# Reading a product's bank before, instead of after, the side work of its period

## Chip, cores and metric

The kernel runs on one core of a Trainium2 chip. The metric is the device time of one launch in microseconds (us). Three runs of the kernel before took 2329.98, 2333.09 and 2333.73 us, median 2333.09.

## What is computed

One layer of a hybrid decoder trunk on a sequence of 2048 tokens of width 1024, all in float32:

```
h = rms_norm(x, pre_norm_w)
p = h @ w_in                       # 1024 x 8320: rwkv, conv, pool, gate columns
y_a = rwkv7_branch(token_shift(p_rwkv, mu_shift), ...)
y_b = b * conv3(c * u) * silu(z)             # p_conv -> b, c, u, z
y_c = mix(window means of u, widths 2..16) * pool_scale * silu(z)
proj = einsum('nbsc,ncd->nbsd', [y_a, y_b, y_c], w_branch)   # 3 x (512 -> 1024)
merged = sum_n sigmoid(p_gate)_n * proj_n
out = x + rms_norm(merged @ w_out, post_norm_w)
```

The rwkv branch is a recurrence over tokens. The kernel solves it in 16 groups of 128 tokens, each with a small triangular inverse.

## The kernel before, in words

The wide matrix products are cut into *products*: one PSUM bank of 128 x 512, twelve TensorE matmuls (four slices of the inner dimension, each as high x high, high x low, low x high halves of a split float32; lines 182 to 184). There are 608 products. Most belong to a `Pair` (lines 189 to 263): two 128-column blocks times two 512-token blocks with seven products instead of eight, called here B11, T1, T2, B21, B22, T3, T4. T4 is postponed and runs inside the next pair, after its T1. There are two `ch` banks and two `mm` banks. B11 is copied out of `ch` by ScalarE (L233), T1 out of `mm` (L238), T2 out of `ch` (L243); B21, B22 and T3 are added by VectorE to these copies (L247, L251, L255). A product may start only when the bank that it writes has been read: T4 needs L255 of T3, two products earlier; T1 of the next pair takes the bank that L247 read.

The weights of a product are split into a high half (ScalarE, `wh`, L141) and a low half (GpSimd, `wl`, L143) a few products ahead, by `supply`; GpSimd also adds weight blocks (L212).

The program runs in *periods*, one to a product: `execute` (lines 1280 to 1299) iterates the job, and at each `yield` behind a product it calls `supply`, issues postponed stores, does one postponed piece of row work (`puts`), and advances the side streams, one step each. Side streams are the rwkv groups, the staging of the second half's operands, the pooled mix, and the splitting of stored activations (`fill`, lines 354 to 358). Only then is the bank read. Each engine works its queue in the order of issue, so the order in which Python issues instructions is the order of each engine's queue.

Names that the prediction needs:
- An rwkv group step by step: G and BK tables; then the *table chain* (L752 to L757), fifteen pairs of small VectorE operations (L754, L755) in four *chunks* over four periods; its result goes to memory and back (L763, L766), is transposed (L771, Td), and TensorE needs Td one period later (L779). VectorE's L794 feeds TensorE's L805 in the same way. L626 belongs to a group's head.
- The merge stage: each product's bank is read by L1015; beside it `fill` (L357 ScalarE, L358 VectorE) prepares later operands.
- The final stage: eight `out_pair`s (lines 1036 to 1073). A row tile needs both its halves: ScalarE squares them (L1049), GpSimd makes the norm (`rstd`, L490 to L492), VectorE scales (L1059) and adds x (L1060). This scaling is postponed through `puts`, except for the T4 half, which is done at once.

Of the kernel before, what the change touches and what calls it, by code (L numbers as in the profile page):

```python
# [53 lines left out]
def trunk_kernel(ctx, tc, x, pre_norm_w, post_norm_w, w_in, mu_shift, rwkv_w0, rwkv_w_up,  # L54
# [39 lines left out]
    def mm_bank():  # L94
        return ps.tile([P, BLK], F32, tag="mm", name="mm", bufs=2)
# [88 lines left out]
            pe.matmul(bank, lo[:, k, :], th[k], start=False, stop=stop and k == HK - 1, skip_group_check=True)  # L184

    sums = [pool]
    tail = [None]

    class Pair:
# [37 lines left out]
        def run(self):  # L227
            ops, sink = self.ops(), self.sink
            ch = chain_bank()
            product(ch, take(), ops["B11"], True)  # L230
            yield
            p1 = work("p1")
            act.copy(p1[:, 16:], ch)  # L233
            bb = mm_bank()
            product(bb, take(), ops["T1"], True)
            yield
            p5 = work("p5")
            act.copy(p5[:, 16:], bb)  # L238
            yield from flush()
            product(ch, take(), ops["T2"], False)  # L240
            yield
            u2 = work("u2")
            act.copy(u2[:, 16:], ch)  # L243
            b2 = mm_bank()
            product(b2, take(), ops["B21"], True)
            yield
            dve.tensor_tensor(p1[:, 16:], p1[:, 16:], b2, ALU.add)  # L247
            sink(0, 0, p1[:, 16:], p1)
            product(bb, take(), ops["B22"], False)
            yield  # L250
            dve.tensor_tensor(u2[:, 16:], u2[:, 16:], bb, ALU.add)  # L251
            sink(0, 1, u2[:, 16:], u2)
            product(ch, take(), ops["T3"], False)
            yield
            dve.tensor_tensor(p5[:, 16:], p5[:, 16:], ch, ALU.add)  # L255
            sink(1, 1, p5[:, 16:], p5)

            def last():
                product(ch, take(), ops["T4"], False)
                yield  # L260
                sink(1, 0, ch, None)

            tail[0] = last
# [25 lines left out]
    def single(ops, c, sink):  # L289

        def body():
            h = ops()
            a1, a2 = take(), take()
            ba, bb = mm_bank(), mm_bank()
            product(ba, a1, h["B11"], True)
            yield
            p1 = work("p1")
            act.copy(p1[:, 16:], ba)  # L298
            product(bb, a1, h["T1"], True, False)
            yield  # L300
            product(ba, a2, h["B21"], False)
            yield
            first = sink(0, ba)
            product(bb, a2, h["B22"], False)
            yield
            dve.tensor_tensor(p1[:, 16:], p1[:, 16:], bb, ALU.add)
            second = sink(1, p1[:, 16:])
            up = take()
            yield from first(up)
            yield from second(up)  # L310

        return Other([w_block(w_in, q, c) for q in range(2)], body)
# [4 lines left out]
    stores, puts = [[], []], []  # L317
# [9 lines left out]
    def after_product():  # L327
        for dst, src in stores.pop(0):
            sp.dma_start(dst, src)
        stores.append([])  # L330
        if puts:
            puts.pop(0)()


    def new_op(o):
# [189 lines left out]
    def rwkv_single(half, h, c):  # L525

        up = []

        def load_up():
            up.append(wp.tile([P, HK, P], F32, tag="ws", name="up", bufs=6))  # L530
            for n, w in enumerate((rwkv_w_up, rwkv_a_up)):
                sp.dma_start(up[0][half_of(n)], w[0].rearrange("k (i n) -> k i n", i=NCT))

        def sink(b, val):
            t0 = half * TH + b * BLK
            sh = rwkv_cols(half, c, b, val)
            th, tl = [wk.tile([P, BLK + 16], F32R, tag="wk", name=t)[:, :BLK] for t in ("th", "tl")]
            act.copy(th, sh)
            dve.tensor_tensor(tl, sh, th.bitcast(F32), ALU.subtract)

            def products(upw):
                (uh, ul) = upw
                for n, bias in enumerate((hw0, ha0)):
                    ns = half_of(n)
                    for i in range(NCT):
                        bank = chain_bank() if i % 2 else mm_bank()
                        pe.matmul(bank, uh[ns, i, :], th[ns], start=True, stop=False)
                        pe.matmul(bank, uh[ns, i, :], tl[ns], start=False, stop=False)
                        pe.matmul(bank, ul[ns, i, :], th[ns], start=False, stop=True)
                        o = work("lo")[:, :BLK]  # L550
                        act.activation(o, bank, AF.Tanh, bias=bias[:, i:i + 1], scale=0.5)
                        store(loraD[n][:, i, t0:t0 + BLK], o)
                        if i == 1:
                            yield
                    yield
            return products

        job = single(h, c * P, sink)
        job.feed.append((load_up, None, lambda: wsplit(up[0])))
        return job  # L560
# [442 lines left out]
    def merge_tile(half, ys, d):  # L1003

        def body():
            acc = [None] * NB
            for n in (1, 2, 0):
                gs = gates()
                w = take()
                turn[0] = not turn[0]  # L1010
                for b in range(NB):
                    bank = mm_bank() if turn[0] else chain_bank()
                    product(bank, w, ys[n, b], True)
                    yield
                    dve.scalar_tensor_tensor(gs[b], gs[b], 1.0, bank, ALU.add, ALU.mult)  # L1015
                    if acc[b] is None:
                        acc[b] = gs[b]
                    else:
                        pool.tensor_tensor(acc[b], acc[b], gs[b], ALU.add)  # L1019
            for b in range(NB):  # L1020
                t0 = half * TH + b * BLK
                store(mD[:, d, t0:t0 + BLK], acc[b])

        return Other([w_block(w_branch[n], 0, d * P) for n in (1, 2, 0)], body)
# [207 lines left out]
    for half in range(2):  # L1232
        side = groups[half]
# [36 lines left out]
    for entry in program:  # L1270
        if isinstance(entry, tuple):
            j = entry[0]
# [7 lines left out]
    def execute(first):  # L1280
        for n, entry in enumerate(program):
            if (n == 0) != first:
                continue
            if not isinstance(entry, tuple):
                entry()
                continue
            j, sides = entry
            if hasattr(j, "begin"):
                j.begin()
            for _ in j.run():  # L1290
                supply(1)
                after_product()
                for side in sides:
                    side.advance()
        if not first:
            for _ in flush():
                after_product()
            while puts or stores[0] or stores[1]:
                after_product()

    with tc.manual_schedule(engines={mybir.EngineType.PE, mybir.EngineType.DVE, mybir.EngineType.Activation,
# [27 lines left out]
```

## Time and profile before

| | |
|---|---|
| median of 3 runs | 2333.09 us |
| profiled run, its own time | 2330.51 us |
| its span | 2328.8 us |
| TensorE busy, share | 2185.9 us, 94% |
| VectorE busy | 1374.5 us, 59% |
| GpSimd busy | 1365.0 us, 59% |
| ScalarE busy | 895.0 us, 38% |
| mean granted TensorE clock | 0.96 |
| share of TensorE in the chain that ended last | 63%, VectorE 14% |

The stages follow each other: preparation up to about 60 us, the first half's products with rwkv groups 0 to 7 up to about 1060 us, the second half's with groups 8 to 15 up to about 1930 us (the merges begin inside it, at about 1838 us), the second half's merges up to 2133 us, the final stage up to the end. The time that counts is TensorE's idle time and the stretches in which its clock is granted at half; the busy shares of the other engines are means over stages.

### The profile page before, as it was taken

The numbers are of one execution on the slowest core, as the hardware profiler recorded it, in microseconds if no ns is written. First come the engines' busy times: TensorE is split into PE (matmuls) and PEld (weight loads), VectorE is DVE, ScalarE is ACT, GpSimd is POOL, SyncE is SP. The second block draws the span as 40 slices with busy tenths as digits, with TensorE's granted clock in tenths as the row PEclk, the third lists the DMA queues.
The fourth block names the chain that finished last, engine by engine and source line by source line (L and its number), as shares of the span: only waits on it lengthen the run. The fifth ranks groups of instructions, "written<-read, shape, count | busy, mean of one in ns | idle before, by whom it ended". The sixth has DMA issues, their size and how long they took to land.

```text
span 2328.8 us, 46956 instructions
## 1 busy us (share of the span) xinstructions
PE 2185.9 (94%) x18514; PEld 1759.5 (76%) x18514; DVE 1374.5 (59%) x2150; ACT 895.0 (38%) x1777; POOL 1365.0 (59%) x1137
## 2 busy tenths in 40 slices
PE   4999999989999999899989999999999999999897
PEld 4788777777787887768877787777877788787775
DVE  7413767676847637534576767846465653526554
ACT  5444433443434436344534433244343511314332
POOL 7657565665656555427656655446565355556775
PEclk7989999999999999979999999999999999999998
DMA  3244313253547427344432323346454765768443
GB/s 103 90 136 129 98 54 95 61 144 107 152 140 209 129 80 236 92 146 138 136 80 62 91 53 113 108 138 186 131 166 118 231 174 170 258 182 275 126 136 104
DMA packets 441207, 313.11 MB, mean 134 GB/s; under 512 B 105557, under 2 KB 362778, under 8 KB 440986
## 3 DMA queue, kind: packets, MB, share of 16 engines
q1 hardware_dynamic: 440986, 310.12, 44.5%
q8 instruction: 145, 2.38, 0.4%
q14 instruction: 76, 0.62, 0.1%
HBM read 206.08 MB, written 103.94 MB: 133 GB/s over the span
## 4 chain that ended last, share of the span: by engine, by line
PE 63%; DVE 14%; issue 5%; POOL 4%; DMA 4%; ACT 3%; SPq 1%; DVEq 0%; POOLq 0%; ACTq 0%
PE ch L182 10%; PE ch L183 9%; PE ch L184 9%; PE mm L182 8%; PE mm L183 7%; PE mm L184 7%; DVE Tt L755 3%; DVE Ttmp L754 3%; PE rk L593 2%; PE rk L711 2%; POOL wl L143 2%; POOL ws L212 1%; PE rk L835 1%; PE rk L827 1%; PE rk L843 1%
## 5 line engine op out<-in xcount | busy, mean ns | idle before, releaser
L143 POOL TENSOR_TENSOR wl<-ws,wh 128x512 fp32r<-128x512 f32 x484 | 674.0, 1395 | 548.1 <-ACT wh L141 514.0
L141 ACT CAST wh<-ws 128x512 fp32r<-128x512 f32 x484 | 298.7, 618 | 253.8 <-PE mm L183 91.3
L182 PE MATMUL ch<-hT,wh 128*128 128x512 f32 x864 | 358.0, 414 | 38.1 <-DVE p L255 30.9
L184 PE MATMUL ch<-hT,wl 128*128 128x512 f32 x864 | 344.8, 399 | 0.3 <-POOL wl L143 0.2
L183 PE MATMUL ch<-lT,wh 128*128 128x512 f32 x864 | 344.9, 399 | 0.1
L182 PE MATMUL mm<-hB,wh 128*128 128x512 f32 x600 | 241.6, 403 | 2.8 <-ACT p L298 2.8
L184 PE MATMUL mm<-hB,wl 128*128 128x512 f32 x600 | 234.3, 390 | 0.7 <-POOL wl L143 0.7
L183 PE MATMUL mm<-lB,wh 128*128 128x512 f32 x600 | 234.3, 391 | 0.0
L182 PEld LDWEIGHTS ch<-hT,wh 128*128 128x128 f32 x864 | 167.5, 194 | 83.3 <-issue 32.6
L143 POOL TENSOR_TENSOR wl<-s,wh 128x512 fp32r<-128x512 f32 x72 | 97.5, 1354 | 217.7 <-ACT wh L141 214.0
L212 POOL TENSOR_TENSOR ws<-ws,s 128x512 f32<-128x512 f32 x144 | 201.7, 1401 | 2.6 <-DMA ws<-in_w_in 2.6
L184 PEld LDWEIGHTS ch<-hT,wl 128*128 128x128 f32 x864 | 166.6, 193 | 38.1 <-POOL wl L143 1.3
L183 PEld LDWEIGHTS ch<-lT,wh 128*128 128x128 f32 x864 | 167.6, 194 | 32.5 <-issue 0.4
L1019 POOL TENSOR_TENSOR g<-g 128x512 f32<-128x512 f32 x64 | 86.4, 1353 | 108.0 <-DVE g L1015 95.9
L182 PEld LDWEIGHTS mm<-hB,wh 128*128 128x128 f32 x600 | 112.6, 188 | 29.7 <-ACT p L298 3.6
L182 PE MATMUL mm<-hT,wh 128*128 128x512 f32 x296 | 124.5, 421 | 10.6 <-DVE p L247 7.0
L184 PEld LDWEIGHTS mm<-hB,wl 128*128 128x128 f32 x600 | 112.7, 188 | 25.8 <-POOL wl L143 1.5
L183 PEld LDWEIGHTS mm<-lB,wh 128*128 128x128 f32 x600 | 112.7, 188 | 21.5
L184 PE MATMUL ch<-hB,wl 128*128 128x512 f32 x288 | 117.7, 409 | 10.5 <-POOL wl L143 10.5
L182 PE MATMUL ch<-hB,wh 128*128 128x512 f32 x288 | 120.8, 419 | 6.8 <-DVE g L1015 4.0
L755 DVE TENSOR_TENSOR Tt<-Tt,Ttmp 128x120 f32<-128x120 f32 (+14 forms) x240 | 117.4, 489 | 8.3
L184 PE MATMUL mm<-hT,wl 128*128 128x512 f32 x296 | 119.9, 405 | 1.0 <-POOL wl L143 0.8
(269 smaller groups left out, 4638.7 us busy)
## 6 DMA issues: line engine op xcount, KB each, us to landing
ws<-in_w_in SPq DMA_DIRECT2D x260, 256.0 KB
g<-gD SPq DMA_DIRECT2D x96, 256.0 KB
gD<-p SPq DMA_DIRECT2D x48, 256.0 KB
ly<-yD SPq DMA_DIRECT2D x48, 256.0 KB
ws<-in_w_branch SPq DMA_DIRECT2D x48, 256.0 KB
mD<-g SPq DMA_DIRECT2D x32, 256.0 KB
ws<-mD SPq DMA_DIRECT2D x32, 256.0 KB
xr<-in_x SPq DMA_DIRECT2D x32, 256.0 KB
```

The source lines that it names most:

```text
L141: act.copy(hi, src)
L143: pool.tensor_tensor(lo, src, hi.bitcast(F32), ALU.subtract)
L182: pe.matmul(bank, hi[:, k, :], th[k], start=start and k == 0, stop=False, skip_group_check=True)
L183: pe.matmul(bank, hi[:, k, :], tl[k], start=False, stop=False, skip_group_check=True)
L184: pe.matmul(bank, lo[:, k, :], th[k], start=False, stop=stop and k == HK - 1, skip_group_check=True)
L212: sums[0].tensor_tensor(w[o], w[a], w[b], op)
L593: both(lambda h, hs: pe.matmul(bank[hs, a * 64:a * 64 + 64], src[hs, a], ident[hs, hs], start=True, stop=True))
L711: both(lambda h, hs: pe.matmul(bgs[n][hs, i * P:(i + 1) * P], BK[hs, n, 2 * i + c], XA[hs, 2 * i + c].rearrange("p x t -> p (x t)"), start ...
L754: dve.tensor_tensor(tmp[:, :, :n], bc(NBt[:, j, j + 1:], 1, 8), bc(Tt[:, :, j], 2, n), ALU.mult)
L755: dve.tensor_tensor(Tt[:, :, j + 1:], Tt[:, :, j + 1:], tmp[:, :, :n], ALU.add)
L827: both(lambda h, hs: pe.matmul(r3[hs, i], G[hs, 1, 0, a], vt[hs, a], start=True, stop=False, skip_group_check=True))
L1019: pool.tensor_tensor(acc[b], acc[b], gs[b], ALU.add)
```

## The change

`yield READ` is put behind each reading of a bank. `execute` now takes two kinds of yields: behind a product it calls `supply` and issues postponed stores, as before; behind the reading it advances the side streams and does one postponed piece of row work. At the end, the loop that empties `puts` does so outside `after_product`, and the two yields of the last T4 do nothing.

```diff
+    READ = True
...
             p1 = work("p1")
             act.copy(p1[:, 16:], ch)
+            yield READ
             bb = mm_bank()
             product(bb, take(), ops["T1"], True)
             yield
...
             yield
             dve.tensor_tensor(p5[:, 16:], p5[:, 16:], ch, ALU.add)
+            yield READ
             sink(1, 1, p5[:, 16:], p5)
 
             def last():
                 product(ch, take(), ops["T4"], False)
                 yield
+                yield READ
                 sink(1, 0, ch, None)
...
         stores.append([])
-        if puts:
-            puts.pop(0)()
...
-                    else:
+                    yield READ
+                    if acc[b] is not gs[b]:
                         pool.tensor_tensor(acc[b], acc[b], gs[b], ALU.add)
...
-            for _ in j.run():
-                supply(1)
-                after_product()
-                for side in sides:
-                    side.advance()
+            for read in j.run():
+                if read:
+                    for side in sides:
+                        side.advance()
+                    if puts:
+                        puts.pop(0)()
+                else:
+                    supply(1)
+                    after_product()
         if not first:
             for _ in flush():
-                after_product()
+                pass
             while puts or stores[0] or stores[1]:
+                if puts:
+                    puts.pop(0)()
                 after_product()
```

The order of instructions on TensorE, GpSimd and the DMA queue is the same as before; only VectorE's and ScalarE's queues change. In the changed kernel the lines are shifted: L247, L251, L255 are L252, L257, L262; L754 and L755 are L767 and L768; L771 is L784; L1059 and L1060 are L1073 and L1074.

VectorE in the final stage, from one pair's B21 (first row) to the next T4's half (last two rows), before:

```order
L247 TENSOR_TENSOR p_22748<-p_22748,mm 128x512
L251 TENSOR_TENSOR u_22820<-u_22820,mm 128x512
L1059 SCALAR_TENSOR_TENSOR p_22748<-p_22748,so,post 128x512
L1060 TENSOR_TENSOR xr<-xr,p_22748 128x512
L255 TENSOR_TENSOR p_22771<-p_22771,ch 128x512
L1059 SCALAR_TENSOR_TENSOR u_22820<-u_22820,so,post 128x512
L1060 TENSOR_TENSOR xr<-xr,u_22820 128x512
L1059 SCALAR_TENSOR_TENSOR o<-ch,so,post 128x512
L1060 TENSOR_TENSOR xr<-xr,o 128x512
```

The same pair with the change:

```order
L252 TENSOR_TENSOR p_22746<-p_22746,mm 128x512
L257 TENSOR_TENSOR u_22818<-u_22818,mm 128x512
L262 TENSOR_TENSOR p_22771<-p_22771,ch 128x512
L1073 SCALAR_TENSOR_TENSOR p_22746<-p_22746,so,post 128x512
L1074 TENSOR_TENSOR xr<-xr,p_22746 128x512
L1073 SCALAR_TENSOR_TENSOR u_22818<-u_22818,so,post 128x512
L1074 TENSOR_TENSOR xr<-xr,u_22818 128x512
L1073 SCALAR_TENSOR_TENSOR o<-ch,so,post 128x512
L1074 TENSOR_TENSOR xr<-xr,o 128x512
```

The reading of T3's bank (L255, now L262) has moved in front of the first postponed scaling.

VectorE at the end of the program, the last pair from T3 on, before:

```order
L255 TENSOR_TENSOR p_23109<-p_23109,ch 128x512
L1059 SCALAR_TENSOR_TENSOR u_23154<-u_23154,so,post 128x512
L1060 TENSOR_TENSOR xr<-xr,u_23154 128x512
L1059 SCALAR_TENSOR_TENSOR o<-ch,so,post 128x512
L1060 TENSOR_TENSOR xr<-xr,o 128x512
L1059 SCALAR_TENSOR_TENSOR p_23109<-p_23109,so,post 128x512
L1060 TENSOR_TENSOR xr<-xr,p_23109 128x512
```

And with the change:

```order
L262 TENSOR_TENSOR p_23109<-p_23109,ch 128x512
L1073 SCALAR_TENSOR_TENSOR p_23086<-p_23086,so,post 128x512
L1074 TENSOR_TENSOR xr<-xr,p_23086 128x512
L1073 SCALAR_TENSOR_TENSOR o<-ch,so,post 128x512
L1074 TENSOR_TENSOR xr<-xr,o 128x512
L1073 SCALAR_TENSOR_TENSOR u_23152<-u_23152,so,post 128x512
L1074 TENSOR_TENSOR xr<-xr,u_23152 128x512
L1073 SCALAR_TENSOR_TENSOR p_23109<-p_23109,so,post 128x512
L1074 TENSOR_TENSOR xr<-xr,p_23109 128x512
```

The scaling of the second half row (`u`) has moved behind the one that waits for T4 (`o`).

VectorE at the start of group 14's table chain, in the pair with T3's reading L255, before:

```order
L251 TENSOR_TENSOR u_18428<-u_18428,mm 128x512
L754 TENSOR_TENSOR Ttmp<-NB,Tt 128x8x15
L755 TENSOR_TENSOR Tt<-Tt,Ttmp 128x8x15
L754 TENSOR_TENSOR Ttmp<-NB,Tt 128x8x14
L755 TENSOR_TENSOR Tt<-Tt,Ttmp 128x8x14
L754 TENSOR_TENSOR Ttmp<-NB,Tt 128x8x13
L755 TENSOR_TENSOR Tt<-Tt,Ttmp 128x8x13
L754 TENSOR_TENSOR Ttmp<-NB,Tt 128x8x12
L755 TENSOR_TENSOR Tt<-Tt,Ttmp 128x8x12
L255 TENSOR_TENSOR p_18334<-p_18334,ch 128x512
```

And with the change:

```order
L257 TENSOR_TENSOR u_18395<-u_18395,mm 128x512
L672 TENSOR_TENSOR d<-d,gst 128x512
L262 TENSOR_TENSOR p_18310<-p_18310,ch 128x512
L767 TENSOR_TENSOR Ttmp<-NB,Tt 128x8x15
L768 TENSOR_TENSOR Tt<-Tt,Ttmp 128x8x15
L767 TENSOR_TENSOR Ttmp<-NB,Tt 128x8x14
```

The reading of T3's bank now stands in front of the chain's first chunk.

## Rows read from the trace of the kernel before

**Rows 1.** Waits of TensorE: in total us, times, longest us

```profile
PE ch L182 <- DVE p L255: 30.9, 13, 5.4
PE rk L779 <- DVE Td L771: 10.8, 5, 3.8
PE rk L805 <- DVE T L794: 9.5, 5, 5.8
PE mm L182 <- DVE p L247: 7.0, 2, 3.5
```

**Rows 2.** Timeline, VectorE, final stage: start, us, operation, [idle before <-releaser]

```profile
2177.89 0.67 DVE L251 TENSOR_TENSOR u<-u,mm 128x512 f32<-128x512 f32 x1
2181.78 1.77 DVE L1059 SCALAR_TENSOR_TENSOR p<-p,so,post 128x512 f32<-128x512 f32 x1 [3.21 <-POOL so L492]
...
2185.14 0.67 DVE L255 TENSOR_TENSOR p<-p,ch 128x512 f32<-128x512 f32 x1
```

**Rows 3.** Timeline, TensorE, T4 of the second out pair

```profile
2185.96 0.52 PE L182 MATMUL ch<-hT,wh 128*128 128x512 f32 x1 [2.62 <-DVE p L255]
```

**Rows 4.** Timeline, GpSimd, the two idle times of the following cycle

```profile
2187.23 1.28 POOL L143 TENSOR_TENSOR wl<-s,wh 128x512 fp32r<-128x512 f32 x1 [2.56 <-ACT wh L141]
...
2201.77 1.30 POOL L143 TENSOR_TENSOR wl<-ws,wh 128x512 fp32r<-128x512 f32 x1 [2.55 <-ACT wh L141]
```

**Rows 5.** Windows: length, busy us (count) PE, PEld, DVE, ACT, POOL; clock; DMA

```profile
2208.39:2230.78 22.39, 19.64 (x84) 15.61 (x85) 11.63 (x12) 7.92 (x19) 16.96 (x17) 1.00 0.49 141
2311.89:2328.80 16.91, 4.36 (x13) 3.19 (x12) 6.36 (x10) 2.52 (x8) 1.87 (x6) 0.72 0.20 75
```

**Rows 6.** Timeline, VectorE, the end

```profile
2311.38 0.68 DVE L251 TENSOR_TENSOR u<-u,mm 128x512 f32<-128x512 f32 x1
...
2315.64 0.68 DVE L255 TENSOR_TENSOR p<-p,ch 128x512 f32<-128x512 f32 x1
...
2325.00 0.69 DVE L1060 TENSOR_TENSOR xr<-xr,p 128x512 f32<-128x512 f32 x1
```

**Rows 7.** Timeline, TensorE, the last T4

```profile
2316.47 0.77 PE L182 MATMUL ch<-hT,wh 128*128 128x512 f32 x1 [4.58 <-DVE p L255]
```

**Rows 8.** Timeline, VectorE, around L626 in a group's head

```profile
247.91 1.76 DVE L626 TENSOR_TENSOR f<-f,k 128x512 f32<-128x512 f32 x1
```

**Rows 9.** Timeline, TensorE, the T4 behind it

```profile
250.42 0.47 PE L182 MATMUL ch<-hT,wh 128*128 128x512 f32 x1 [3.37 <-DVE p L255]
```

**Rows 10.** Timeline, VectorE, group 0's chain in the convolution's pairs

```profile
299.12 0.68 DVE L247 TENSOR_TENSOR p<-p,mm 128x512 f32<-128x512 f32 x1
...
302.91 0.68 DVE L255 TENSOR_TENSOR p<-p,ch 128x512 f32<-128x512 f32 x1
```

**Rows 11.** Timeline, TensorE, T1 and then T4 behind them

```profile
299.94 0.77 PE L182 MATMUL mm<-hT,wh 128*128 128x512 f32 x1 [3.52 <-DVE p L247]
...
305.20 0.54 PE L182 MATMUL ch<-hT,wh 128*128 128x512 f32 x1
```

**Rows 12.** Timeline, VectorE, group 14's chain: first operation, last operation, Td

```profile
1777.65 0.58 DVE L754 TENSOR_TENSOR Ttmp<-NB,Tt 128x120 f32<-128x120 f32 x1
...
1797.73 0.17 DVE L755 TENSOR_TENSOR Tt<-Tt,Ttmp 128x8 f32<-128x8 f32 x1
...
1805.00 0.71 DVE L771 STREAM_TRANSPOSE Td<-TT 128x512 f32<-128x512 f32 x1 [4.70 <-DMA TT<-td]
```

**Rows 13.** Timeline, TensorE: T3's last matmul there, and the matmuls on Td

```profile
1779.29 0.39 PE L184 MATMUL ch<-hT,wl 128*128 128x512 f32 x1
...
1805.77 0.75 PE L779 MATMUL rk<-Td,G 16*32 16x32 f32 x64 [2.27 <-DVE Td L771]
```

**Rows 14.** Timeline, VectorE, splitting activations during the merges

```profile
2005.10 5.78 DVE L358 TENSOR_TENSOR ly<-ly,hy 128x512 fp32r<-128x512 f32 x4
```

**Rows 15.** Timeline, TensorE, the merge product behind it

```profile
2011.61 0.47 PE L182 MATMUL mm<-hy,wh 128*128 128x512 f32 x1 [3.29 <-DVE g L1015]
```

**Rows 16.** Line L754: operation, xcount, duration ns min/median/max, first and last start

```profile
L754 DVE TENSOR_TENSOR Ttmp<-NB,Tt x240: 172/243/1381, 278.0 to 1888.2; 128x120 f32<-128x120 f32 x8, 128x104 f32<-128x104 f32 x8, 128x88 f32<-128x88 f32 x8, 128x72 f32<-128x72 f32 x8
```

More of the change, by code (lines that the diff above doesn't have):

```diff
@@ L251, in run @@
             dve.tensor_tensor(u2[:, 16:], u2[:, 16:], bb, ALU.add)
+            yield READ
             sink(0, 1, u2[:, 16:], u2)
@@ L255, in run @@
             dve.tensor_tensor(p5[:, 16:], p5[:, 16:], ch, ALU.add)
+            yield READ
             sink(1, 1, p5[:, 16:], p5)
@@ L260, in last @@
                 yield
+                yield READ
                 sink(1, 0, ch, None)
@@ L298, in body @@
             act.copy(p1[:, 16:], ba)
+            yield READ
             product(bb, a1, h["T1"], True, False)
             yield
+            yield READ
             product(ba, a2, h["B21"], False)
             yield
+            yield READ
             first = sink(0, ba)
@@ L306, in body @@
             dve.tensor_tensor(p1[:, 16:], p1[:, 16:], bb, ALU.add)
+            yield READ
             second = sink(1, p1[:, 16:])
@@ L554, in products @@
                             yield
+                            yield READ
                     yield
+                    yield READ
             return products
@@ L1017, in body @@
                         acc[b] = gs[b]
-                    else:
+                    yield READ
+                    if acc[b] is not gs[b]:
                         pool.tensor_tensor(acc[b], acc[b], gs[b], ALU.add)
```

## The prediction, made before the changed kernel was run

> **What bounds the kernel now.** I read the page's engine shares, then TensorE's waits, then for each wait the timeline of the engine that released it. TensorE is busy nearly throughout, so only its idle time and its half-clock stretches can change. Of its waits on other work the largest is for VectorE's L255, the reading of T3's bank: 30.9 us in 13 waits; L247 adds 7.0. The side work's own waits are of the same kind: 10.8 us for Td and 9.5 us for L794 [rows 1]. The change concerns both lists, with opposite signs: a bank is read sooner by one step of side work, and a side step starts later, because it stands behind a reading that cannot begin before its product ends. An addition that reads a bank takes 0.68 us.
>
> **Final stage (forecast: 21 us less).** Here the postponed scaling stands in front of L255 and VectorE waits in it: L251 is done at 2178.56, then VectorE idles 3.21 us for GpSimd's norm, scales, adds, and reads T3's bank only at 2185.14 [rows 2]; T4 stands still for 2.62 us [rows 3]. T3 itself had ended before: TensorE had run two more products and was out of work. With the change L255 follows L251 directly, at about 2178.6, 6.6 us sooner, and T4 finds its bank free.
>
> What is late next is GpSimd. In a cycle of 22.39 us it is busy 16.96 us [rows 5], and it idles twice: 2.56 us before the low half of T2's weights and 2.55 us before that of T1's [rows 4]. The first comes from ScalarE, which waits in its queue with the square of L255's result; this idle time goes with the early L255. The second hangs on L247, which stands behind T4's norm and four scalings and additions of VectorE; the change leaves that chain alone. So the cycle becomes 22.39 - 2.56 = 19.8 us. TensorE's seven products need 19.64 us at full clock [rows 5], so the two limits lie close together and the cycle cannot shrink further. There are seven T4 inside the stage. The first saves its wait, about 2.6 us like [rows 3]; each of the six cycles behind it saves 2.5 us: 2.6 + 15.0 = 17.6 us.
>
> The end: L251 is done at 2312.06, L255 could end at 2312.74, and T4 start 0.15 us later, as it does after L255 now (2316.32 to 2316.47): 2312.9 instead of 2316.47 [rows 6, 7], 3.6 us less. Those twelve matmuls are busy 4.36 us, at a clock of 0.72 over the window [rows 5]; after a wait of under 1 us I take the rate of the full-clock row (19.64 / 7 = 2.8 us): 1.5 us less. Against this stands the scaling of one half row, which now runs after T4 instead of beside it. A scaling and an addition take 0.74 + 0.69, so 1.4 us more: the last addition [rows 6] has one more pair in front of it. Sum of the stage: 17.6 + 3.6 + 1.5 - 1.4 = 21.3, taken as 21. Bounds: if GpSimd's second idle time grows by most of what the first loses, a cycle saves 1 us and the stage 2.6 + 6 + 3.6 + 1.5 - 1.4 = 12; if the half clock in the other cycles goes too (about 1.7 us in each of three), 26.
>
> **Readings that nothing late follows (10 us less).** In the two halves' group heads L626 (1.76 us) stands in front of L255, and T4 waits 3.37 us [rows 8, 9]; there is one such place in either half. L255 moves ahead by 1.7 us, twice: 3.4 us. Of the 9.5 us on L794 one wait of 5.8 stays (nothing in front of it moves); the other four, 3.7 us, come from ScalarE or VectorE standing in a side step while a reading and what follows it queue behind, and I let them go. Three smaller ones of the same kind, in the single columns and behind them, I estimate at 1 us each. Together 10; bounds 3 (L626 alone) and 16 (the half clock behind those waits gone as well).
>
> **Readings inside a table chain (nothing).** Group 0's third chunk stands in front of L247, and T1 waits 3.52 us until L247 ends at 299.80 [rows 10, 11]. With the change L247 comes some 2.5 us sooner, at the chunk's place. But VectorE has no idle time there, and in front of L255 stands the same work in both orders: it still ends at about 303.6, and T4, which started at 305.20 [rows 11] after a T1 that ran at half clock, now waits for it. The wait moves from T1 to T4. Four more waits in the convolution and pool pairs have this form. A gain of up to 2 us in each is possible, as is a loss of 1.
>
> **Side work behind a reading (12 us more).** Group 14 is the example. Its chain starts at 1777.65, inside T3's period; T3's last matmul starts at 1779.29 [rows 12, 13] and ends some 0.4 us later. With the change L255 is read first, from about 1779.8 to 1780.5, and the chain starts 2.8 us later. L255 no longer stands between first and second chunk (0.7 us), so the chain's end, 1797.90, slips by about 2 us. Behind it is a round trip through memory: Td starts 7.1 us after the end, VectorE waits 4.70 us for it, and TensorE already waits 2.27 us for Td [rows 12, 13]. So TensorE pays the 2 us in full. I find six of the sixteen chains whose first chunk stands in a period with a VectorE reading and starts before the product's end: 6 x 2 = 12 us. Five chains make TensorE wait now [rows 1], which is the cover for this slip in the others: where Td is ready a microsecond or two early, part of it is hidden. Where no hold occurs a side step slips by one reading (0.68 us) at most. Bounds: 5 us (half the slip hidden, no other), and 27 us (below, the third rival).
>
> A rule bears on the length of the chunks. An operation of a chunk takes 243 ns in the median, but up to 1381 ns [rows 16]; its neighbours in time are GpSimd's operations of about 1.3 us [rows 4]. The Trainium skill, "SBUF — State Buffer", section "Who interferes with whom", says that a VectorE instruction with two SBUF inputs and a GpSimd instruction that reads SBUF exclude each other, and the one that starts first holds the port to its end. The trace agrees: additions with a bank as one input stay at 0.68 us, chunk operations are stretched fivefold. By this rule a chunk that is moved to just behind the product's end, when the splitting of the next weights begins, would meet more of GpSimd's operations. It speaks against the change, and is part of the third rival.
>
> **Merges (2 us less).** Four splittings of 5.78 us stand in front of the reading on which a product waits 3.29 us [rows 14, 15]. The reading comes first now; but the splittings themselves, from which TensorE takes operands three products later, start 0.7 us later, and the next reading stands behind them. I keep 2 us; bounds: 5 less, 3 more.
>
> **Sum.** -21 - 10 + 0 + 12 - 2 = -21 us. The profiled run took 2330.51 us, so 2309.5; it lies 2.6 us under the median of the runs shown, 2333.09, from which I count: 2312 us.
>
> **Rivals.**
> 1. *The early stages gain too.* ScalarE and VectorE stand idle in side steps while a finished bank waits behind them; every such stand ends earlier, and the chains gain what they lose by the hold. Then the 12 us become about zero and a few waits more go: 2312 - 14 = 2298. For it: VectorE's 4.70 us idle before Td with L255 behind it [rows 12]. Against: VectorE has none in the chain stretches.
> 2. *GpSimd takes back the final stage.* The cycle's second idle time grows as the first goes, because T4's norm waits its turn behind the same five weight operations. Then the stage gives 12 us: 2321.
> 3. *The chains lose a product each.* Mechanism: a chunk can no longer use the time of the product in front of its reading, 2.7 us; Td slips by that. The five chains that TensorE waits for now would cost 13.5 us, all sixteen 43; I take ten, 27 us. By the lock of the port, if the moved chunks meet GpSimd more often, it is rather more. This becomes decisive when it exceeds what the final stage and the free readings give: from 33 us on (21 + 10 + 2) the kernel is slower than before. With rival 2's 12 us in place of 21 the point is 24 us, and 27 us of loss give 2333 + 3; with a little more in the chains, 2340. Against it: in ten chains the first chunk stands in a period whose reading is ScalarE's, or starts after the product's end anyway.
>
> **Chances.** Forecast 0.60, rival 1 0.15, rival 2 0.13, rival 3 0.12. A measurement of this kernel can tell about 0.2%, 4.7 us. Faster by more: 0.58 of the forecast, all of rival 1, 0.09 of rival 2: 0.82. Within: 0.02 + 0.04 + 0.02 of rival 3 = 0.08. Slower: 0.10. The range goes from rival 1 (2298) to 2329: the final stage at its lower bound of 12 and the chains at 20 in place of 12 give 2312 + 9 + 8; rival 3 beyond it is left out, and the tail of rival 1.
>
> **What would show it.** In the profile of the changed kernel: no wait of T4 for the successor of L255 in the final stage, cycles from T4 to T4 of 19.8 to 20.3 us, GpSimd with one idle time in each; the last T4 waiting under 1 us, and two scalings behind its own at the end. TensorE's waits for Td grown from 10.8 to some 20 us. In group 0 a wait before T4 in place of that before T1. I am wrong if the final cycles stay above 21.5 us (rival 2), if the waits for Td exceed 35 us (rival 3), or if they do not grow (rival 1).

## Result, and the profile after

The changed kernel took 2343.08 us (median of 6 runs, 2338.62 to 2345.73), the kernel before 2331.53 us in the runs beside it: ratio 1.0051, 95% interval 1.0033 to 1.0070. The change costs about 12 us where 21 us less were forecast. The profiled run took 2345.73 us, 15.2 us more than that of before.

Where the time went can be read from the starts of products. The last `mm` product of the merges started at 2111.25 us before and starts at 2136.74 now; the last T4 started at 2316.47 [rows 7] and starts at 2331.67. So the stages up to the merges lose 25.5 us, the final stage gives 10.3 us back, and from the last T4 to the end it is 12.3 us both times. TensorE's waits after (total us, times, longest), to be held against [rows 1]:

```profile
PE rk L792 <- DVE Td L784: 29.1, 7, 10.5
PE ch L184 <- POOL wl L143: 17.7, 12, 6.6
...
PE ch L182 <- DVE p L262: 10.4, 4, 4.5
PE rk L818 <- DVE T L807: 10.2, 5, 4.6
...
PE ch L182 <- DVE Ttmp L767: 5.0, 1, 5.0
```

The wait for T3's reading fell from 30.9 to 10.4 us. Nearly all of the fall is the final stage's. The early stages had 12.4 us of it and have 9.1 under this name; besides, the longest of their waits, 5.43 us for the T4 at 1501.73, is still there with 5.03 us at 1501.13, put down to L767 by the profile (last row). The wait for Td rose from 10.8 to 29.1, and seven new waits for GpSimd's `wl`, 0.94 us each, stand in the final stage. The loss sits in three places: the products behind the Td of groups 11, 13 and 15. The windows of these products, before and then after (columns as in [rows 5]):

```profile
1515.35:1526.86 11.51, 7.70 (x177) 6.35 (x176) 7.19 (x12) 6.97 (x17) 5.95 (x6) 0.85 0.53 157
1708.99:1724.97 15.98, 13.62 (x265) 10.71 (x264) 7.51 (x12) 10.36 (x24) 8.15 (x8) 1.00 0.47 149
1894.73:1901.85 7.12, 7.12 (x153) 5.52 (x151) 1.97 (x3) 1.00 (x2) 3.78 (x3) 1.00 0.86 225
```

```profile
1514.65:1534.92 20.27, 9.76 (x175) 7.92 (x176) 10.40 (x14) 7.88 (x18) 8.32 (x8) 0.66 0.52 158
1716.84:1743.90 27.06, 18.70 (x264) 14.91 (x264) 9.52 (x14) 13.11 (x29) 11.29 (x9) 0.75 0.56 170
1912.83:1926.71 13.88, 10.00 (x153) 7.50 (x152) 2.70 (x5) 1.00 (x2) 5.03 (x4) 0.75 0.83 236
```

8.76 + 11.08 + 6.76 = 26.60 us; the rest of the early stages gives 1.1 us back. By these rows TensorE's idle time in the three windows grew by 16.6 us, and the other 10.0 us are the same matmuls taking longer: those of the second window are busy 13.62 us at a granted clock of 1.00 and 18.70 us at 0.75. A stretch at the lower level, 1.2 GHz, follows each of the four standstills of over 3 us there.

In group 13 the chain's fourth chunk shows what made Td late. VectorE and then GpSimd, before (start, us, operation):

```profile
1696.29 0.17 DVE L754 TENSOR_TENSOR Ttmp<-NB,Tt 128x24 f32<-128x24 f32 x1
...
1697.35 0.17 DVE L755 TENSOR_TENSOR Tt<-Tt,Ttmp 128x8 f32<-128x8 f32 x1
```

```profile
1697.62 1.29 POOL L143 TENSOR_TENSOR wl<-ws,wh 128x512 fp32r<-128x512 f32 x1 [2.50 <-ACT wh L141]
```

And after:

```profile
1706.77 0.68 DVE L262 TENSOR_TENSOR p<-p,ch 128x512 f32<-128x512 f32 x1
1707.37 0.91 DVE L767 TENSOR_TENSOR Ttmp<-NB,Tt 128x24 f32<-128x24 f32 x1
...
1708.73 1.29 DVE L768 TENSOR_TENSOR Tt<-Tt,Ttmp 128x16 f32<-128x16 f32 x1
1710.06 1.21 DVE L767 TENSOR_TENSOR Ttmp<-NB,Tt 128x8 f32<-128x8 f32 x1
1711.30 1.23 DVE L768 TENSOR_TENSOR Tt<-Tt,Ttmp 128x8 f32<-128x8 f32 x1
```

```profile
1708.70 1.29 POOL L143 TENSOR_TENSOR wl<-s,wh 128x512 fp32r<-128x512 f32 x1 [0.47 <-PE mm L184]
1709.95 1.29 POOL L214 TENSOR_TENSOR ws<-ws,s 128x512 f32<-128x512 f32 x1
1711.20 1.30 POOL L143 TENSOR_TENSOR wl<-ws,wh 128x512 fp32r<-128x512 f32 x1
```

Before, six operations take 1.2 us in a gap of GpSimd's work (it idles 2.50 us up to 1697.62). After, they stand behind L262 and take 5.2 us, since three of them each last about as long as the GpSimd operation beside them.

The same window has a second wait. ScalarE's cast for the pooled mix (L970) waits 9.03 us for a store of the gate that still reads its target tile, VectorE's step on it (L972) waits with it, and T (L807, before the change L794), which TensorE needs, stands behind that step (ScalarE, VectorE, TensorE, after):

```profile
1733.74 0.62 ACT L970 CAST ph<-pl 128x512 fp32r<-128x512 f32 x1 [9.03 <-DMA gD<-gate]
```

```profile
1734.39 0.69 DVE L972 TENSOR_TENSOR pl<-pl,ph 128x512 fp32r<-128x512 f32 x1 [9.39 <-ACT ph L970]
```

```profile
1736.08 0.31 PE L818 MATMUL rk<-T,G 32*32 32x32 f32 x2 [3.29 <-DVE T L807]
```

Before, the cast waited 0.29 us for that store and T kept TensorE 1.85 us. The product that starts at 1714.52 before and at 1729.79 after, in front of this wait, is 7.4 of the 11.1 us late; the other 3.7 come behind it.

In group 11 it is ScalarE. Before, the copy of T2 (L243) waited 1.21 us for a store that still read its target tile, and the side steps stood in front of it:

```profile
1518.50 0.59 ACT L243 COPY u<-ch 128x512 f32<-128x512 f32 x1 [1.21 <-DMA yD<-silu]
```

Now they stand behind it (ScalarE, then VectorE, then TensorE, after):

```profile
1519.58 0.59 ACT L247 COPY u<-ch 128x512 f32<-128x512 f32 x1 [5.28 <-DMA yD<-silu]
...
1522.05 0.62 ACT L970 CAST ph<-pl 128x512 fp32r<-128x512 f32 x1 [0.56 <-POOL pwl L968]
```

```profile
1522.70 1.09 DVE L972 TENSOR_TENSOR pl<-pl,ph 128x512 fp32r<-128x512 f32 x1 [6.52 <-ACT ph L970]
1523.72 0.67 DVE L252 TENSOR_TENSOR p<-p,mm 128x512 f32<-128x512 f32 x1
1524.32 0.70 DVE L784 STREAM_TRANSPOSE Td<-TT 128x512 f32<-128x512 f32 x1
```

```profile
1525.16 1.08 PE L792 MATMUL rk<-Td,G 16*32 16x32 f32 x64 [10.51 <-DVE Td L784]
```

A store of the pool stage (`yD<-silu`) holds the copy, the copy holds the pooled mix's cast, VectorE waits 6.52 us for the cast, and Td, whose row shows no wait for its own data, stands behind it.

The final stage: a cycle fell from 22.39 us [rows 5] to 21.15, not to 19.8. Its window, GpSimd's remaining idle time with three other operations of the cycle, and VectorE beside them:

```profile
2273.66:2294.81 21.15, 19.70 (x84) 15.62 (x84) 13.68 (x12) 7.94 (x19) 18.25 (x18) 1.00 0.48 144
```

```profile
2274.50 1.74 POOL L143 TENSOR_TENSOR wl<-s,wh 128x512 fp32r<-128x512 f32 x1
2276.20 1.73 POOL L214 TENSOR_TENSOR ws<-ws,s 128x512 f32<-128x512 f32 x1
...
2280.84 1.29 POOL L143 TENSOR_TENSOR wl<-ws,wh 128x512 fp32r<-128x512 f32 x1
...
2290.40 1.29 POOL L143 TENSOR_TENSOR wl<-ws,wh 128x512 fp32r<-128x512 f32 x1 [2.55 <-ACT wh L141]
```

```profile
2275.01 1.78 DVE L1073 SCALAR_TENSOR_TENSOR u<-u,so,post 128x512 f32<-128x512 f32 x1
...
2283.22 0.75 DVE L1073 SCALAR_TENSOR_TENSOR o<-ch,so,post 128x512 f32<-128x512 f32 x1 [4.74 <-POOL so L503]
...
2284.91 1.77 DVE L1073 SCALAR_TENSOR_TENSOR p<-p,so,post 128x512 f32<-128x512 f32 x1
2286.72 1.67 DVE L1074 TENSOR_TENSOR xr<-xr,p 128x512 f32<-128x512 f32 x1
2288.32 0.68 DVE L252 TENSOR_TENSOR p<-p,mm 128x512 f32<-128x512 f32 x1
```

One idle time of GpSimd is gone, as forecast. But it is busy 18.25 us a cycle instead of 16.96: six of its eleven wide operations take about 1.74 us instead of 1.29, where three did before. 18.25 and 2.55 and some 0.35 of small gaps make 21.15. The scaling of the half row u and the addition behind it explain it; they ran in GpSimd's idle time before and run beside three of its operations now (line of all eight scalings: busy, mean ns), before and after:

```profile
L1059 DVE SCALAR_TENSOR_TENSOR u<-u,so,post 128x512 f32<-128x512 f32 x8 | 5.9, 741 | 0.0
```

```profile
L1073 DVE SCALAR_TENSOR_TENSOR u<-u,so,post 128x512 f32<-128x512 f32 x8 | 13.2, 1647 | 0.0
```

### The profile page after: what moved, and what is told of

It reads as the page before. It is cut to its first block, busy times and chain, and to the rows that moved or that the text cites. A ratio compares the mean times of both kernels' runs of the same rounds, so it can differ in the third digit from the quotient of the medians.

```text
span 2344.0 us, 46992 instructions
## 1 busy us (share of the span) xinstructions
PE 2189.2 (93%) x18514; PEld 1759.0 (75%) x18514; DVE 1402.5 (60%) x2150; ACT 897.8 (38%) x1777; POOL 1383.0 (59%) x1137
## 5 line engine op out<-in xcount | busy, mean ns | idle before, releaser
L182 PE MATMUL ch<-hT,wh 128*128 128x512 f32 x864 | 355.0, 411 | 21.2 <-DVE p L262 10.4
L143 POOL TENSOR_TENSOR wl<-s,wh 128x512 fp32r<-128x512 f32 x72 | 104.8, 1456 | 178.8 <-ACT wh L141 175.3
L768 DVE TENSOR_TENSOR Tt<-Tt,Ttmp 128x120 f32<-128x120 f32 (+14 forms) x240 | 119.5, 498 | 8.2
```

The source lines that it names most:

```text
L143: pool.tensor_tensor(lo, src, hi.bitcast(F32), ALU.subtract)
L182: pe.matmul(bank, hi[:, k, :], th[k], start=start and k == 0, stop=False, skip_group_check=True)
L768: dve.tensor_tensor(Tt[:, :, j + 1:], Tt[:, :, j + 1:], tmp[:, :, :n], ALU.add)
```

## Experiments

Each run in the table was timed beside the kernel before; the ratio is to that kernel, with its 95% interval, since its own median moved between 2327.9 and 2332.7 us from one set to the next. 0.1% is 2.3 us. A time in one trace is one execution: the kernel before and sides_in_front, whose VectorE order is the same up to the final stage, lie up to 5 us apart at single products.

| run | median us | ratio |
|---|---|---|
| the change | 2343.08 | 1.0051 [1.0033, 1.0070] |
| sides_in_front | 2316.88 | 0.9934 [0.9919, 0.9950] |
| row_work_in_front | 2356.98 | 1.0098 [1.0081, 1.0115] |
| front_of_scalar | 2332.81 | 1.0006 [0.9993, 1.0018] |
| front_of_vector | 2326.35 | 0.9981 [0.9969, 0.9993] |
| behind_first_copies | 2320.69 | 0.9949 [0.9934, 0.9964] |
| chain_in_front | 2320.75 | 0.9955 [0.9938, 0.9972] |
| chain_and_td_in_front | 2314.73 | 0.9932 [0.9914, 0.9950] |
| first_chunk_in_front | 2334.93 | 1.0037 [1.0024, 1.0049] |
| last_chunk_in_front | 2332.05 | 1.0014 [1.0003, 1.0025] |
| after_one_period_more | 2334.57 | 1.0019 [1.0007, 1.0031] |
| t3_row_later | 2305.72 | 0.9885 [0.9866, 0.9904] |
| head_reads_first | 2304.71 | 0.9884 [0.9866, 0.9902] |
| row_later_one_period_more | 2312.34 | 0.9924 [0.9907, 0.9941] |
| chain_front_row_later | 2304.04 | 0.9899 [0.9884, 0.9915] |
| copy_of_t2_last | 2297.99 | 0.9856 [0.9831, 0.9881] |

**The two halves of the change.** In the changed kernel each pair of yields got the kind of its reading: A (B11, T1), U (T2), B, C, T (B21, B22, T3), M (merges), N (nothing read).

```diff
-            yield READ
+            yield "T", True
...
-            for read in j.run():
+            for kind, read in j.run():
+                if not read:
+                    supply(1)
+                    after_product()
+                if read != (kind in FRONT):
+                    for side in sides:
+                        side.advance()
+                if read and puts:
+                    puts.pop(0)()
```

sides_in_front has all kinds in FRONT. row_work_in_front has none there, and does the row work at the product's yield, ahead of the side streams.

> Side streams in front of every reading again, as in the kernel before; the postponed row work stays behind. VectorE's order then differs from before in the final stage alone. Both theories (hold: a chain step now waits for the end of a product; slot: a side step now waits behind a ScalarE copy whose target tile a store still reads) expect the chains as before and the final stage as in the changed kernel, which gained 10 us there by the trace: 2331.5 - 10 = 2321 us, bounds 2317 and 2326. If the 21 us of the prediction were reachable, 2310.

> The other half alone: side streams behind the readings, the postponed row work in front again. The early stages as in the changed kernel, which was 25 us late at the start of the final stage by the trace, the final stage as before: 2331.5 + 25 = 2357 us, bounds 2350 and 2362. If the two halves did not simply add up, nearer to 2343.

Row work alone gives 0.66%, 15 us; side streams alone cost 0.98%, 23 us. The sum, +0.32%, lies just below the interval of the whole. The halves are separate matters: in the trace of sides_in_front the early stages end 1.1 us ahead of before (2110.14 against 2111.25), and the final stage gives 12.1 us; with the row work in front the final stage gives nothing.

**Which readings.** front_of_scalar has FRONT = A, U; front_of_vector has B, C, T, M.

> Side streams in front of ScalarE's copies (B11, T1, T2), behind VectorE's readings (B21, B22, T3, merges). Hold: the chains lose as in the changed kernel, 2343 (bounds 2338 to 2348). Slot: the wait of 10.5 us for group 11's Td goes back to about 4 and the half clock behind it with it; the others stay: 2343 - 8 = 2335 us.

> The reverse: side streams in front of VectorE's readings and of the merges', behind ScalarE's copies. Hold: the chains are as before, 2321 us (bounds 2316 to 2327). Slot: group 11's wait of 10.5 us for Td stays, and only that: 2321 + 8 = 2329 us.

Against sides_in_front, standing behind VectorE's readings costs 0.72% (17 us), behind ScalarE's copies 0.47% (11 us). Together 1.19%, about the 1.17% of all. Neither theory holds alone. The trace of front_of_vector shows group 11 as in the changed kernel (ScalarE, then TensorE):

```profile
1520.09 0.58 ACT L247 COPY u<-ch 128x512 f32<-128x512 f32 x1 [5.91 <-DMA yD<-silu]
```

```profile
1525.07 1.07 PE L792 MATMUL rk<-Td,G 16*32 16x32 f32 x64 [8.66 <-DVE Td L784]
```

In front_of_scalar group 11's wait for Td is 6.79 us, less than the 10.51 of the changed kernel and more than the 3.81 of before. Group 13 parts into its two waits: behind VectorE's readings only (front_of_scalar) it waits 4.37 us for Td and under 0.8 for T, behind ScalarE's copies only (front_of_vector) under 0.8 for Td and 5.29 for T.

behind_first_copies (FRONT without A) takes the copy of T2 out of it:

> Side streams behind ScalarE's copies of B11 and T1 alone, in front of the copy of T2 (u) and of all of VectorE's readings. The run with sides in front took 2316.9, the one behind all of ScalarE's copies 2326.4 us. Slot theory: the 9.5 us are the copy of T2, whose target tile is still read by a store in groups 11 and 13: 2317 to 2319 us here. If any side step behind a ScalarE copy costs alike, two thirds of it: 2323.

0.9949 lies between the two expectations and doesn't decide; its trace does for group 11, where the same wait is 3.68 us:

```profile
1517.20 0.74 PE L792 MATMUL rk<-Td,G 16*32 16x32 f32 x64 [3.68 <-DVE Td L784]
```

**Which side steps.** The changed kernel, with the rwkv stream stepped in front while it is in a stretch. The tail of the group before steps in the same stream and moves with it, and so does the head of the next group in the runs that reach up to Td:

```diff
+        chain[0] = True
         yield from step()
         for j in range(15):
...
+        chain[0] = False
         yield from step(1, True)
...
                 else:
                     supply(1)
                     after_product()
+                    early = [side for side in sides if side in groups and chain[0]]
+                    for side in early:
+                        side.advance()
```

In chain_and_td_in_front `chain[0] = False` stands behind Td's transpose; in the runs of one chunk it is true for that chunk alone.

> The changed kernel (2343.1 us), but an rwkv group steps in front of the reading while it is in its table chain: the four chunks L767, L768 and nothing else. Hold (the first chunk waits behind a reading of VectorE's, and its fourth meets the splitting on GpSimd): the losses in groups 13 and 15 go, 5 to 7 us each with the half clock, group 11's stays: 2343 - 12 = 2331 us, bounds 2325 and 2336. If the chunks are not what is late, 2343.

> The same, and the steps up to Td (L784) are in front as well: td, TT, Td. By hold and slot together the whole loss of the side streams but that of the steps behind Td: group 11's 8 us go too, as Td no longer stands behind the copy of T2 that waits for a store: 2320 us, bounds 2316 and 2326. If Td is late for something else that stands in front of it (the mixing step's L972), 2329, as with the chunks alone.

The four chunks, with the tail's steps beside them, give back 0.96% (22 us), more than expected: group 13's wait of 4.83 us for Td is gone and group 15's falls from 3.88 to 0.98. Group 13's wait for T stays (3.74 us), and so does group 11's for Td (TensorE, total, times, longest):

```profile
PE rk L796 <- DVE Td L788: 17.1, 7, 9.1
```

With td, TT and Td in front as well the time is that of sides_in_front (0.9932, 0.9934), but by another sum. At the T2 of the second pool pair in the second half (1419.21 before, 1416.37 with sides in front) this run is at 1408.98: the readings that came forward gave some 7 to 10 us by then. Group 11 takes 5 of them back, as Td there still waits 7.4 us: the mixing step L972 (L976 in this run) stands behind the copy of T2 and in front of Td. The second theory for Td in the expectation is right for this group, though not in its total.

> The changed kernel (2343.1 us) with the first chunk of a chain alone in front of the reading. First-chunk theory, as the prediction had it: nearly what all four chunks gave, 2320.8; 2322 to 2326 us. Last-chunk theory: the chain's end, from which the round trip through memory starts, is set by the last chunk, behind the reading of its own period: 2338 to 2343.

> The changed kernel with the last chunk alone in front. Last-chunk theory: most of the 22 us, 2323 to 2328. First-chunk theory: 2338 to 2343. If each chunk gives a part, both runs lie at 2330 to 2337.

The first chunk gives 0.14%, which the intervals don't tell from nothing, the last 0.37%, all four 0.96%: the third case of the expectation. The last counts for more than the first, and neither alone for half. That the rest arises at the two chunks between, each behind the reading of its own period, is likely but not shown; no run has them alone.

**The slack of the round trip.** `step(3 if g < 8 else 2)` before Td became `step(3)`.

> The changed kernel, with a third period between the loading of TT and Td in groups 8 to 15 too (groups 0 to 7 have three, 8 to 15 two). By the traces the changed kernel lost 25 us in groups 11, 13 and 15 and nothing in the first half. Slack theory: that is because the chains of the second half have a period less for the round trip through memory; with it their waits for Td (29.1 us in all) fall to a few us, and the half clock behind them goes: 2343 - 22 = 2321 us. Other theory: side steps behind a reading are late as such, and the first half is spared for another reason; then the waits move to T (L807) and what follows, and the time stays at 2340 or above.

0.32% back, not the 0.9% expected: 2334.57 us lies between the two theories. Waits for Td fell from 29.1 to 7.9 us, but those for T rose from 10.2 to 19.9 and those for the copy L247 from 4.7 to 10.6. Slack is a part of it, and what the extra period costs elsewhere eats some.

**The final stage.** t3_row_later: sides in front, and no row work behind U, B, C.

```diff
-                if read and puts:
+                if read and kind not in ("U", "B", "C") and puts:
                     puts.pop(0)()
```

> Side streams in front as before (2316.9 us by the run with sides in front), and no postponed row work behind the readings of T2, B21 and B22: T3's scaling of the pair before now comes behind T3's reading and no longer stands between T4's scaling and the reading of B21. Theory A, the loop (T4's norm on GpSimd, four VectorE operations, B21's reading, its square, ScalarE's wh, GpSimd's wl) sets the 21.15 us of a cycle: GpSimd's second idle time of 2.55 us goes, the cycle falls to 19.8 (TensorE's 19.7), seven times 1.35 = 9 us less, 2307 to 2308. Theory B, GpSimd's own work, stretched to 18.25 us beside VectorE, sets it: the idle time only moves, the cycle stays at 21.1 and the time at 2317.

Theory A holds, and the gain is 0.49%, 11 us, against sides_in_front. A cycle:

```profile
2218.34:2237.49 19.15, 19.15 (x86) 15.78 (x85) 11.85 (x12) 8.15 (x19) 18.81 (x18) 1.00 0.51 165
```

TensorE is busy without a gap, and GpSimd's busy time of 18.81 us fits in, as it no longer waits. This version beats both kernels, the one before by 1.15%.

scaling_on_scalar asks for the price of the two engines side by side:

```diff
-                    dve.scalar_tensor_tensor(o, val, ss[e][:, 3:4], post[0][:, es], ALU.mult, ALU.mult)
+                    act.activation(o, val, AF.Copy, scale=ss[e][:, 3:4])
```

> Leaves out the product with the post norm weights: the scaling of the final stage is one ScalarE operation with the norm as scale in place of VectorE's operation with two inputs in SBUF; sides in front. Asks how much of GpSimd's 18.25 us a cycle comes from VectorE beside it. Port theory: GpSimd's operations of 1.74 us that ran beside the scalings fall to 1.29; four to six of eleven in a cycle are long now, about three would be, GpSimd busy near 17.0 us. Other theory (the long ones are long by what they compute): busy stays at 18.2.

The kernel is otherwise sides_in_front, where GpSimd is busy 18.25 us in a cycle of 21.14. Here the cycle is 19.14, as in t3_row_later, and GpSimd is busy 17.48 us:

```profile
2218.39:2237.53 19.14, 19.14 (x86) 15.77 (x85) 6.21 (x8) 10.79 (x22) 17.48 (x18) 1.00 0.56 172
```

GpSimd's work didn't change, only what ran beside it: 0.8 us less than in sides_in_front, 1.3 less than in t3_row_later. The 17.0 of the port theory are not reached; VectorE's additions still run beside it. As the kernel leaves out the post norm weights, its time says nothing on the change.

**Joining the parts.** head_reads_first is t3_row_later with the side stream behind T3's reading in the last rwkv pair; row_later_one_period_more is t3_row_later with the third period; chain_front_row_later joins chain_and_td_in_front with the final stage of t3_row_later.

> As the run with T3's row work later, and in the last rwkv pair of either half alone the side stream behind T3's reading, where L639 of a group's head (1.76 us) stood in front of the reading that T4 waits for. The changed kernel gained 3 us at either place by its trace: 6 us less than the run beside it. If the head's slip is given back by its chain, as the hold theory says of chain steps, no difference.

> The run with T3's row work later (2305.7 us) with the same third period in groups 8 to 15. Its waits for Td are 12.4 us, five of them in the second half, each with a half-clock stretch of 3.4 us behind it that costs about 1.7. Slack theory: 9 to 15 us less, 2293. Other theory: the group that ends a period later lacks it at its own end, 2304 to 2310.

> The run with the chain and Td in front (2314.7 us), with the postponed row work not behind the readings of T2, B21 and B22, which gave 11 us in the final stage: 2303 us if they add up. By its trace the chain and Td in front leave the early stages 5 us ahead of the run with all sides in front: then 2300.

The wait behind L626 (now L639) shrinks, but the time does not (0.9884 against 0.9885): a gain of 2 to 6 us was expected and can't be told from none. The third period costs 0.39% where the chains were not late. The joined version is as fast as t3_row_later, within both intervals. Its loss in group 11 was tried last, with all side streams in front at T2:

```diff
-            yield
+            yield FRONT
             u2 = work("u2")
...
-                    early = [side for side in sides if side in groups and chain[0]]
+                    early = [side for side in sides if read == FRONT or side in groups and chain[0]]
```

> As chain_front_row_later (0.9899 of the kernel before; 2304.0 us), and at T2 all side streams step in front of its copy. If group 11's Td is late because the mixing step stands behind that copy, the wait of 7 us for Td falls to about 4 or less, and the time by 4 to 5 us: 2299 us, 0.988 of before. If not, Td still waits 7 us and the time stays.

0.9856, 0.43% under the run without it, and group 11's wait for Td is down from about 7 to 3.79 us, as expected (TensorE):

```profile
1513.23 0.74 PE L796 MATMUL rk<-Td,G 16*32 16x32 f32 x64 [3.79 <-DVE Td L787]
```

The waits for T fell from 10.5 to 5.0 us, as group 13's of 3.71 is gone too. Against the run without it the trace gains 4.1 us in group 11 and 3.2 in group 13, but stands 7.3 us later in front of both; why is open.

This is the best version, 1.44% under the kernel before. It keeps the change's idea (readings first) and exempts what the traces showed: the chain up to Td, the copy that waits for a store, and the row work in front of B21's reading.

## Why the prediction was wrong

- **Side work behind a reading: the step that failed.** Forecast 12 us; putting the chains and Td back in front gave 1.19%, 28 us. The mechanism, a chain that slips behind a VectorE reading so that TensorE waits for Td, is there. Three things were wrong in its sizing. First, the rule that chose six chains: the first chunk. Group 14, the example, started 2.7 us later, as worked out: 1799.27 against 1777.65 [rows 12], with the 18.9 us taken off by which the products around it are late already. But its chain ended at 1816.57 against 1797.90, 18.7 us: on time. It lost nothing (VectorE, after, reading, first and last operation):

```profile
1798.66 0.69 DVE L262 TENSOR_TENSOR p<-p,ch 128x512 f32<-128x512 f32 x1 [1.33 <-PE ch L184]
1799.27 0.28 DVE L767 TENSOR_TENSOR Ttmp<-NB,Tt 128x120 f32<-128x120 f32 x1
...
1816.40 0.17 DVE L768 TENSOR_TENSOR Tt<-Tt,Ttmp 128x8 f32<-128x8 f32 x1
```

  Group 13's chain, with the 7.9 us of its own neighbours taken off, started 0.8 us later and ended 7.2 us later; 3.9 of these came in its fourth chunk. Second, only VectorE's readings were counted; a ScalarE copy, which may wait for a store, holds side steps as well: 11 us in front_of_vector, seen in group 11 and in group 13's wait for T. Third, 2 us per chain left out the clock: in the three windows above 10.0 of the 26.6 us are matmuls at the lower level behind a wait.
- **Final stage.** Forecast 21, measured 10.3 to 12.1 in the traces. That L255 goes in front and T4's wait with it was right, as was the shape of the end (a wait of 1.29 us where under 1 was said, and two scalings at the end). The mis-sized term is GpSimd's busy time, held at 16.96 us and measured at 18.25: 1.3 us more, which with the 19.8 forecast make the 21.1 us of a cycle. The mechanism of the second idle time was named rightly, as what the change leaves alone; t3_row_later shows that the loop through it was the bound. The forecast's other limit, TensorE's 19.64 us, was none: the cycle fell to 19.15 there.
- **Readings that nothing late follows.** Forecast 10 us less, of these the changed kernel has little left: at the B22 in front of group 11's Td it is 0.7 us ahead (1511.77 against 1512.47). T4 at L626 did start earlier, at 246.84 against 250.42 [rows 9], 3.6 us where 1.7 were counted. The size of the term was about right: with the chains and Td in front the readings that come forward give 7 to 10 us, though no run tells which of them. The chains up to there ate it: where that run stands at 1408.98, the changed kernel stands at 1419.01 and before at 1419.21.
  With the three terms as measured, -12 in the final stage, about -7 to -10 here and +28 for the chains, the change comes to +6 to +9; 12 were measured, with an interval of 8 to 16.
- **Readings inside a table chain.** Forecast nothing. In group 0 the wait moved as said: T1 waits 1.69 us instead of 3.52 [rows 11], T4 behind it 2.33 instead of none.
- **Merges.** Forecast 2 us less, measured 0.6 more (24.9 us late behind group 15's chain, 25.5 at the last merge tile), within the bounds.
- **Rivals and chances.** In numbers rivals 2 and 3 came together: the final stage at its 12 us and the chains at 28, where rival 3 had 27. Its own sum named this case (2340 us), but at 0.12, as if the two were unlikely together. In mechanism neither came as told, so the match is in part luck: GpSimd's second idle time stayed at 2.55 us and its busy time grew, and not ten chains lost a product each, but three groups most of it. The signs of being wrong named neither: the final cycle of 21.15 us is under 21.5, and the waits for Td, 29.1 us, are under 35, since a sign on waits alone leaves out the clock behind them.
  The row that spoke for a larger loss was in hand, [rows 16]: a chunk's operation takes 243 ns or 1381. The Trainium skill, "SBUF — State Buffer", section "Who interferes with whom", explains it by a port that only one of the two engines holds; the trace agrees with group 13's fourth chunk, 5.2 us beside GpSimd and 1.2 alone, and scaling_on_scalar with 0.8 us of GpSimd's time against its base. This stretching enters both mis-sized terms; it was weighed for the chains only, and for GpSimd's cycle not at all.

What stays open: how the 22 us of the chunks split into plain lateness and stretching by GpSimd, and what of them belongs to the tail's steps that moved along. The first two stand in group 13, and no run took one away alone.

## What to carry to other kernels

Work that is moved behind a wait takes over everything that wait depends on, a store that still holds a target tile too; look at the end of a chain, not at its start, and at what lies between its end and the engine that needs it. Two changes in one edit can have opposite signs: here one was worth 15 us and the other cost 23, and splitting the edit by its two lists was the first experiment that told. Before counting an idle stretch of an engine as saved, ask what ran in it beside that engine and will now run against it.

## What the runs showed of the hardware

VectorE and GpSimd slow each other in step: beside each other a scaling (0.74 us alone) takes 1.78 us and a GpSimd operation (1.29 alone) 1.74, and GpSimd starts the next one 1.70 us later, less than the 2.03 us of one after the other. A VectorE operation of 0.17 us becomes one of 1.2. VectorE operations with one input in a bank aren't stretched (L252, L262: 0.67 to 0.69 us in every row above, at 1706.77 beside GpSimd too). TensorE's seven products take 19.64 us busy with small waits between them [rows 5] and 19.15 without any.
